# A feed-forward block whose up projection goes by seven products of halves, with the down projection as a stage of its own

## The chip, the cores and the metric

The kernel runs on one core of a Trainium2 chip. The metric is the device time of one execution in microseconds (us). TensorE (PE) multiplies, VectorE (DVE), ScalarE (ACT) and GpSimd (POOL) do the elementwise work, SyncE (SP) issues most DMAs. Each engine runs its own queue in order and waits on semaphores for the others.

## The reference

One layer of a bidirectional RWKV-7 and mLSTM trunk, on 128 context tokens and 1024 latent tokens, which the kernel handles as 1152 columns. The change is in the last part of the layer alone, the gated feed-forward; all before it (modulation, input projection, the two scans, branch and output projections) computes the same as it did.

```
h = rmsnorm(x, norm_g[2]) * (1 + sc2) + sh2                  # (tokens, 1024)
u_act, u_val = split(h @ ffn_up, 2)                          # ffn_up (1024, 2 * 2816)
u_act = dwconv_grid(u_act, ffn_conv) + ffn_conv_b            # 3x3 on a 16x64 grid; width 3 on the context
f = (silu(u_act) * u_val) @ ffn_down                         # ffn_down (2816, 1024)
x = x + g2 * rmsnorm(f, norm_g[3])
```

## The kernel before

The 1152 tokens are 9 blocks of 128, and 3 groups of 384 columns. All large products are made with numbers split in two: `hi` is the value rounded to the matmul's format (an ACT copy), `lo` is what is left (a subtraction on DVE), and a product is hi·hi + hi·lo + lo·hi, three matmuls where one would stand (`mm_split`). `split_w` (L366 to L382) loads a weight tile and makes its two parts.

The output projection (`wo`, L1456 to L1493) takes the blocks one after another: 48 matmuls into two PSUM banks, then a norm, the residual, a second norm, eight transposes, and `modulate` (L1434 to L1454), which writes the hi and lo parts of h, channel-major, into `AS`, where the feed-forward reads them.

The feed-forward has 22 blocks of 128 hidden features. For each block `up_act` (L1510 to L1524) makes 3 x 24 matmuls of 384 columns, two ACT evacuations per group, the convolution on DVE (`conv_taps`, L34 to L50: eight shifted multiply-adds over the grid, "taps", and two small ones over the context), and SiLU on ACT. `up_val` (L1526 to L1536) makes the other 3 x 24 matmuls, multiplies them on DVE straight from PSUM with the activated half, and splits the result into `f2`. The down projection runs in rounds of one to three blocks: 9 token blocks x 2 halves, three matmuls of 512 columns for each block of the round, added to `acc` in SBUF by DVE (L1597). In the last round POOL multiplies `acc` by the gate row (L1599), and norm, residual and output follow. Eight small modulation products (`mod_cols`) stand between the rounds.

A scheduler sets each engine's order from dependencies and program order, except where the code holds an engine to program order (`pe.on`, `v.on`). POOL has nothing to do in the feed-forward until the last round.

## Time and profile before

| | us |
|---|---|
| median of 3 runs (range) | 2232.75 (2231.03 to 2235.47) |
| the profiled execution | 2232.55 |
| its span | 2230.8 |
| last matmul of the output projection starts | 1388.50 |
| last matmuls of the feed-forward start | 2219.47 |

The span runs from the first to the last instruction of the profiled execution; the 1.75 us between it and that execution's time lie outside. The feed-forward is what follows 1388.7 us. In the rows below, busy time of PE and of its weight loads (PEld) overlap, and a matmul's length in a row is longer than its distance from the next, since matmuls are pipelined: rates are read from start to start.

### The profile page before, as it was taken

What the parts mean: (1) busy time and instruction counts of PE and PEld (TensorE: products, weight loads), DVE (VectorE), ACT (ScalarE), POOL (GpSimd) and SP (SyncE); (2) the same over time, 40 slices, a digit from 0 to 9 for tenths busy, and PEclk for the clock granted to TensorE, in tenths of its full rate; (3) what the DMA queues carried; (4) which work ended last, traced back from release to release, by engine and by line L of the source; (5) the groups of instructions that cost most, each with busy time, mean ns of one, the idle gap of its engine ahead of it and who ended that gap; (6) DMA issues with size and microseconds to landing.
All of it is one profiled execution on the core that took longest, in us unless ns stands there. A gap on an engine that the chain in (4) does not pass through costs nothing. (4 is left out here: it accounts for less than half of the span.)

```text
span 2230.8 us, 39173 instructions
## 1 busy us (share of the span) xinstructions
PE 2086.4 (94%) x16051; PEld 1926.7 (86%) x16051; DVE 1372.8 (62%) x2131; ACT 819.8 (37%) x1595; POOL 567.0 (25%) x726
## 2 busy tenths in 40 slices
PE   6999998998988988879879999999999999999998
PEld 4998998988877877869868888999999999999996
DVE  4766678879744656653733465665575556565658
...
GB/s 268 54 87 127 113 128 106 154 120 138 158 133 139 127 133 133 104 212 214 197 242 194 201 188 75 49 57 57 38 48 57 48 48 48 57 39 47 39 57 170
DMA packets 370803, 256.63 MB, mean 115 GB/s; under 512 B 90529, under 2 KB 345669, under 8 KB 370624
## 3 DMA queue, kind: packets, MB, share of 16 engines
...
## 5 line engine op out<-in xcount | busy, mean ns | idle before, releaser
L395 PE MATMUL pg<-act,whi 128*128 128x384 f32 (+1 forms) x3808 | 727.0, 338 | 0.5 <-DVE act L358 0.4
L395 PEld LDWEIGHTS pg<-act,whi 128*128 128x128 f32 (+1 forms) x3808 | 667.6, 188 | 12.9 <-DVE act L358 0.8
L395 PE MATMUL pg<-act,wlo 128*128 128x384 f32 (+1 forms) x1904 | 373.8, 336 | 5.1 <-DVE wlo L382 5.1
L395 PEld LDWEIGHTS pg<-act,wlo 128*128 128x128 f32 (+1 forms) x1904 | 333.4, 187 | 8.6 <-DVE wlo L382 5.4
L382 DVE TENSOR_TENSOR wlo<-wraw,whi 128x1024 fp32r<-128x1024 f32 x130 | 164.2, 1264 | 227.8 <-ACT whi L381 222.1
L47 DVE SCALAR_TENSOR_TENSOR ua<-uraw,par,ua 128x945 f32<-128x945 f32 (+2 forms) x176 | 215.0, 1221 | 39.2 <-ACT ua L1519 36.0
L1599 POOL TENSOR_TENSOR x<-facc,grow 128x512 f32<-128x512 f32 x16 | 23.5, 1488 | 809.1 <-DMA x<-x1d 799.0
L395 PE MATMUL pfd<-whi,f 128*128 128x512 f32 x792 | 226.1, 394 | 0.2 <-ACT f L1533 0.2
L381 ACT ACTIVATE whi<-wraw 128x1024 fp32r<-128x1024 f32 x130 | 136.7, 1053 | 156.4 <-PE pg L395 85.3
L395 PEld LDWEIGHTS pfd<-whi,f 128*128 128x128 f32 x792 | 147.0, 188 | 28.9 <-issue 1.6
L1597 DVE TENSOR_TENSOR facc<-pfd,facc 128x512 f32<-128x512 f32 x162 | 110.8, 690 | 50.5 <-PE pfd L395 50.5
L542 POOL TENSOR_TENSOR Lb<-Lb,tmp 96x31 f32<-96x31 f32 (+15 forms) x155 | 129.4, 835 | 12.2
L540 POOL TENSOR_TENSOR tmp<-La,Lb 96x31 f32<-96x31 f32 (+15 forms) x155 | 121.9, 787 | 28.7 <-DMA La<-Ad 16.9
L395 PE MATMUL pfd<-wlo,f 128*128 128x512 f32 x396 | 122.7, 391 | 0.0
L1523 ACT ACTIVATE ua<-ua 128x1152 f32<-128x1152 f32 x22 | 25.7, 1168 | 221.8 <-DVE ua L47 221.8
L1533 ACT ACTIVATE f<-ua 128x384 fp32r<-128x384 f32 x66 | 32.0, 518 | 192.9 <-DVE ua L1532 192.9
L69 PE MATMUL pg<-act,whi 128*128 128x384 f32 x496 | 99.3, 349 | 0.0
L1467 PE MATMUL pwo<-whi,act 128*128 128x512 f32 x288 | 90.1, 392 | 1.1 <-ACT whi L381 1.1
L874 DVE TENSOR_TENSOR KA<-psc,msk 64x512 f32<-64x512 f32 x72 | 49.3, 684 | 67.2 <-ACT A L873 66.0
L47 DVE SCALAR_TENSOR_TENSOR qacc<-zraw,par,qacc 128x945 f32<-128x945 f32 (+2 forms) x64 | 84.4, 1319 | 9.5 <-ACT qacc L598 9.0
L395 PEld LDWEIGHTS pfd<-wlo,f 128*128 128x128 f32 x396 | 74.3, 188 | 16.5
L69 PEld LDWEIGHTS pg<-act,whi 128*128 128x128 f32 x496 | 87.3, 194 | 1.1
...
## 6 DMA issues: line engine op xcount, KB each, us to landing
...
```

Of the source, the lines that this page charges most:

```text
L47: v.scalar_tensor_tensor(o, img[:, r0 + i:r1 + i, c0 + j:c1 + j], wt, o, op0=ALU.mult, op1=ALU.add)
L69: return (lambda *a, **k: tc.keep_in_program_order(f(*a, **k))) if self.on else f
L381: s.activation(hi, raw, AF.Copy)
L382: v.tensor_tensor(lo, raw, hi.bitcast(F32), op=ALU.subtract)
L395: pe.matmul(out, wt(hw, k), at(ha, k), start=(i == 0), stop=(i == last))
L540: e.tensor_tensor(t3, L[:, j, i].unsqueeze(2).to_broadcast([NI, n, m]), X[:, j:j + 1, c].to_broadcast([NI, n, m]), op=ALU.mult)
L542: e.tensor_tensor(X[:, i, c], X[:, i, c], t3, op=ALU.subtract)
L874: v.tensor_tensor(q.KA[orr, :, h, :], sc_[h][orr], msk[orr, d:d + 1, :].to_broadcast([64, 4, 128]), op=ALU.mult)
L1467: pe.matmul(pts[b][q], AS[g][:, ha, k, 128 * o:128 * o + 128], wo2[k][hw][:, 0, 512 * q:512 * q + 512], start=(k == 0 and i == 0), stop=(k ...
L1523: s.activation(ua, ua, AF.Silu)
L1533: s.activation(f2[:, 0, gs], ua[:, gs], AF.Copy)
L1597: v.tensor_tensor(acc[:, b, qs], pt, acc[:, b, qs], op=ALU.add)
```

## The change

The last step of the output projection no longer writes hi and lo parts but stores h itself in memory (`h2d`). From there the feed-forward loads it in two chunks of 576 tokens. Each chunk is one step of Strassen's recursion in Winograd's form: h is cut into four quarters (two halves of the channels, two of the tokens, 288 columns each), the weights of a feature block into four (two halves of the channels; the activation and the value features), and seven products P1 to P7 of quarters or of their sums and differences stand in place of eight. The operand sums on the token side (T1 to T4) are made once for all blocks; those on the weight side are made on POOL for every block; the output sums are made by DVE and POOL as the products leave PSUM. Every product ("unit") is 12 matmuls of 288 columns.

The convolution runs as before, a step after each unit. The product of the two halves is made on POOL, and stored to memory (`f2d`) from POOL's queue. When all blocks are done, the down projection runs in three sweeps of 384 tokens that keep their sums in PSUM: it loads f back from `f2d` (`f_group`), splits it, and loads `ffn_down` (13 of its 22 row blocks in every sweep, the other 9 once). The eight `mod_cols` move into the output projection, and all eight PSUM banks belong to the units.

```diff
+    h2d = dram("h2d", [2, 128, 4, T])
+    f2d = dram("f2d", [NFB, 128, T])
...
+    def x_load(c, q, t, dst):
+
+        o = 2 * TH * c + TH * t
+        dma(f32(dst), h2d[q][:, :, o:o + TH])
...
+    def x_split(c, nm, raw, hi, lo):
+        s.activation(hi, f32(raw), AF.Copy)
+        v.tensor_tensor(lo, f32(raw), f32(hi), op=ALU.subtract)
+        X[nm, c] = (hi, lo)
...
+    def x_sub(e, out, a, b):
+        e.tensor_tensor(out, f32(a), f32(b), op=ALU.subtract)
+        return out
...
-            hi = AS[g][:, 0, 4 * q:4 * q + 4, 128 * o:128 * o + 128]
-            lo = AS[g][:, 1, 4 * q:4 * q + 4, 128 * o:128 * o + 128]
-            s.activation(hi, hf, AF.Copy)
-            (v if b == NB - 1 else gp).tensor_tensor(lo, hf, hi.bitcast(F32), op=ALU.subtract)
-
-    with tc.tile_pool(name="wo", bufs=1) as wop, tc.tile_pool(name="wot", bufs=2) as wt:
+            dma(h2d[q][:, :, 128 * b:128 * b + 128], hf)
...
+                modulate(ob, b)
+                if b > 0:
+
+                    for _ in mod_cols(128 * (39 + b), 128, (8,), aw_, wt, pss):
+                        pass
+            if b == 5:
+
+                x0 = actp.tile([128, 6144], F32R, name="x0", tag="act0")
+                x1 = actp.tile([128, 6144], F32R, name="x1", tag="act1")
+                r11, r12, r21, r22, x22l = (quarter(x0, i) for i in range(5))
+                x11h, x11l, x21h, x21l, x22h = (quarter(x1, i) for i in range(5))
+                for q, t, r in ((0, 0, r11), (1, 0, r21), (0, 1, r12), (1, 1, r22)):
+                    x_load(0, q, t, r)
+                x_split(0, "X11", r11, x11h, x11l)
+                x_split(0, "X21", r21, x21h, x21l)
+                x_split(0, "X22", r22, x22h, x22l)
+                ta = x_sub(gp, x_tmp(), r12, r11)
+                tb = x_sub(gp, x_tmp(), r22, ta)
...
+    banks(pg=8)
...
+    def x_rest(c, ta, tb, raw, his):
+
+        r11, r12, r21, r22 = raw
+        x_split(c, "T1", ta, his[0], r11)
+        tc_ = x_sub(v, x_tmp(), r22, r12)
+        x_split(c, "T2", tb, his[1], r22)
+        td = x_sub(v, tb, tb, r21)
+        x_split(c, "T3", tc_, his[2], r12)
+        x_split(c, "T4", td, his[3], r21)
+
+    x_rest(0, ta, tb, (r11, r12, r21, r22), [quarter(x2, i) for i in range(4)])
+    q11, q12, q21, q22 = xb[4:8]
+    x_load(1, 0, 0, q11)
+    x_load(1, 1, 0, q21)
+    x_split(1, "X11", q11, xb[1], xb[2])
+    x_split(1, "X21", q21, xb[3], xb[8])
+    x_load(1, 0, 1, q12)
+    x_load(1, 1, 1, q22)
+
+    def x_late():
+        x_split(1, "X22", q22, xb[9], xb[10])
+        ta = x_sub(v, x_tmp(), q12, q11)
+        tb = x_sub(v, x_tmp(), q22, ta)
+        x_rest(1, ta, tb, (q11, q12, q21, q22), [xb[0]] + xb[11:14])
...
+    PROD = ("P1", "P2", "P6", "P7", "P4", "P5", "P3")
+    XOP = dict(P1="X11", P2="X21", P6="T2", P7="T3", P4="T4", P5="T1", P3="X22")
+
+    units = [(0, "P1", 0), (0, "P2", 0), (0, "P1", 1), (0, "P2", 1), (0, "P6", 0), (0, "P7", 0),
+             (1, "P1", 0), (1, "P2", 0), (1, "P1", 1), (1, "P2", 1), (0, "P4", 0), (0, "P5", 0),
+             (0, "P6", 1), (0, "P7", 1), (0, "P4", 1), (0, "P5", 1), (0, "P3", 0), (0, "P3", 1)]
+    units += [(1, m, c) for m in PROD[2:] for c in range(2)]
+    units += [(i, m, c) for i in range(2, NFB) for m in PROD for c in range(2)]
...
+    def w_split(i, m):
+
+        a11, a12, a21, a22 = raws[i]
+        if m == "P1":
+            s1s[i] = wt.tile([128, 4, 128], F32, name="s1", tag="hf", bufs=1)
+        s1 = s1s[i]
+        src = dict(P1=a11, P2=a12, P6=a11, P7=a21, P4=a22, P5=s1, P3=a12)[m]
+        w = hl()
+        s.activation(w[:, 0], src, AF.Copy)
+        (gp if m in ("P5", "P3") else v).tensor_tensor(w[:, 1], src, f32(w[:, 0]), op=ALU.subtract)
+        HLs[i, m] = w
+        if m == "P1":
+            gp.tensor_tensor(s1, a21, a22, op=ALU.add)
+            gp.tensor_tensor(a21, a11, a21, op=ALU.subtract)
+            gp.tensor_tensor(a11, s1, a11, op=ALU.subtract)
+        if m == "P2":
+            gp.tensor_tensor(a12, a12, a11, op=ALU.subtract)
+
...
+        def unit(i, m, c):
+
+            w, x = HLs[i, m], X[XOP[m], c]
+            t1 = slice(2 * TH * c, 2 * TH * c + TH)
+            t2 = slice(2 * TH * c + TH, 2 * TH * c + 2 * TH)
+            pt = psg([128, TH], "pu")
+            n = 0
+            for hw, hx in PARTS:
+                for k in range(4):
+                    pe.matmul(pt, w[:, hw, k], x[hx][:, k], start=(n == 0), stop=(n == 11))
+                    n += 1
+            if m == "P1" and c == 0:
+                acts[i] = cvt("uraw")
+            if m == "P7" and c == 0:
+                vals[i] = cvt("uval")
+            act, val = acts[i], vals.get(i)
+            if m == "P1":
+                s.activation(act[:, t2], pt, AF.Copy)
+            elif m == "P2":
+                s.activation(act[:, t1], pt, AF.Copy)
+                gp.tensor_tensor(act[:, t1], act[:, t1], act[:, t2], op=ALU.add)
+            elif m == "P6":
+                v.tensor_tensor(act[:, t2], pt, act[:, t2], op=ALU.add)
+            elif m == "P7":
+                v.tensor_tensor(val[:, t2], pt, act[:, t2], op=ALU.add)
+            elif m == "P4":
+                v.tensor_tensor(val[:, t1], val[:, t2], pt, op=ALU.subtract)
+            elif m == "P5":
+                v.tensor_tensor(val[:, t2], pt, val[:, t2], op=ALU.add)
+                v.tensor_tensor(act[:, t2], pt, act[:, t2], op=ALU.add)
+            else:
+                v.tensor_tensor(act[:, t2], pt, act[:, t2], op=ALU.add)
...
+        def conv(i):
+
+            raw, val = acts.pop(i), vals.pop(i)
+            ua = cvt("ua")
+            s.activation(ua, raw, AF.Identity, scale=P("ffn_conv", 22 * 4 + i), bias=P("ffn_conv_b", i))
+            yield
+            for _ in conv_taps(v, raw, ua, lambda t: P("ffn_conv", 22 * t + i)):
+                yield
+            s.activation(ua, ua, AF.Silu)
+            gp.tensor_tensor(val, val, ua, op=ALU.mult)
+            pdma(f2d[i], val)
+            yield
...
+        def f_group(sw, j):
+
+            n = min(8, NFB - 8 * j)
+            t_ = actp.tile([128, 2, 8, G3], F32R, name="fg", tag=f"act{(1, 0, 2)[j]}")
+            ts = slice(G3 * sw, G3 * sw + G3)
+            for o in range(0, n, 2):
+                dma(f32(t_[:, 1, o:o + 2]), f2d[8 * j + o:8 * j + o + 2, :, ts].rearrange("k p t -> p k t"))
+                s.activation(t_[:, 0, o:o + 2], f32(t_[:, 1, o:o + 2]), AF.Copy)
+                v.tensor_tensor(t_[:, 1, o:o + 2], f32(t_[:, 1, o:o + 2]), f32(t_[:, 0, o:o + 2]), op=ALU.subtract)
+                yield
...
+        for u, (i, m, c) in enumerate(units):
+            while ns < len(order) and first_of[order[ns]] <= u + 9 and (ns < 6 or last_of[order[ns - 6]] < u):
+                w_split(*order[ns])
+                ns += 1
+                j = nloaded[0]
+                if j < NFB and all((j - 2, p_) in HLs for p_ in PROD):
+                    w_load()
+            if u == 6:
+                x_late()
+            unit(i, m, c)
+            if conving:
+                next(conving, None)
+            if (m, c) == ("P3", 1):
+                if conving:
+                    for _ in conving:
+                        pass
+                conving = conv(i)
+            if (i, m, c) == (NFB - 1, "P7", 1):
+                g0 = f_group(0, 0)
...
+        for sw in range(3):
+            pd = [[psg([128, 512], "pfd") for q in range(2)] for o in range(3)]
...
+            no = NFB - 3 if sw == 0 else NS
+            for k in range(no):
...
+                w = wds.pop(k) if k < NS else res[k]
+                for o in range(3):
                     for q in range(2):
+                        down_mm(pd[o][q], sw, k, o, q, w, k == 0, False)
...
+                    for k in range(no, NFB):
+                        down_mm(pd[o][q], sw, k, o, q, res[k], False, k + 1 == NFB)
+                    out_half(b, q, pd[o][q], ob, ss)
...
+                out_norm(b, x, ob, ss)
```

POOL, first before, then now. Before, its last rows are the gate products of the branch merge (L1415), the lo parts of h in the output projection (L1454) and the gate products of the last round (L1599):

```order
L1415 TENSOR_TENSOR sg_13402<-sg_13402,sg_13404 128x384 x3
L1454 TENSOR_TENSOR act_160<-hf,act_160 128x4x128 x6
L1454 TENSOR_TENSOR act_161<-hf,act_161 128x4x128 x6
L1454 TENSOR_TENSOR act_162<-hf,act_162 128x4x128 x4
L1599 TENSOR_TENSOR x_20292<-facc,grow 128x512 x6
L1599 TENSOR_TENSOR x_20293<-facc,grow 128x512 x6
L1599 TENSOR_TENSOR x_20294<-facc,grow 128x512 x4
```

Now one block's period in the middle of the feed-forward reads so (`hl` are the hi and lo parts of a weight quarter, `s` and `wraw` the weight quarters and their sums, `uraw` and `uval` the two halves of the block's outputs):

```order
L1623 TENSOR_TENSOR hl<-s_15709,hl 128x512
L1626 TENSOR_TENSOR s_15956<-wraw 128x512
L1627 TENSOR_TENSOR wraw<-wraw 128x512
L1623 TENSOR_TENSOR hl<-wraw,hl 128x512
L1658 TENSOR_TENSOR uraw<-uraw 128x288 x2
L1628 TENSOR_TENSOR wraw<-s_15956,wraw 128x512
L1630 TENSOR_TENSOR wraw<-wraw 128x512
L1680 TENSOR_TENSOR uval<-uval,ua 128x1152
L1681 DMA f2d<-uval 128x1152
```

POOL has ten instructions in every block of the feed-forward, where it had none.

DVE, first before, a stretch between two rounds (`facc` is the down projection's sum):

```order
L47 SCALAR_TENSOR_TENSOR ua<-uraw,par,ua 128x15x63
L47 SCALAR_TENSOR_TENSOR ua<-uraw,par,ua 128x16x63 x2
L47 SCALAR_TENSOR_TENSOR ua<-uraw,par,ua 128x15x63
L47 SCALAR_TENSOR_TENSOR ua<-uraw,par,ua 128x960
L47 SCALAR_TENSOR_TENSOR ua<-uraw,par,ua 128x15x63
L1532 TENSOR_TENSOR ua<-pg,ua 128x384 x3
L1534 TENSOR_TENSOR f_16144<-ua,f_16144 128x384 x3
L382 TENSOR_TENSOR wlo<-wraw,whi 128x1024
L50 SCALAR_TENSOR_TENSOR ua<-uraw,par,ua 128x127 x2
L382 TENSOR_TENSOR wlo<-wraw,whi 128x1024
L47 SCALAR_TENSOR_TENSOR ua<-uraw,par,ua 128x15x63
L266 TENSOR_TENSOR modT<-pmt,par 128x2
```

and now, from the last of a block's output sums on (`pu` is PSUM):

```order
L1669 TENSOR_TENSOR uraw<-pu,uraw 128x288 x2
L47 SCALAR_TENSOR_TENSOR ua<-uraw,par,ua 128x15x63
L50 SCALAR_TENSOR_TENSOR ua<-uraw,par,ua 128x127
L47 SCALAR_TENSOR_TENSOR ua<-uraw,par,ua 128x960
L50 SCALAR_TENSOR_TENSOR ua<-uraw,par,ua 128x127
L47 SCALAR_TENSOR_TENSOR ua<-uraw,par,ua 128x15x63
L47 SCALAR_TENSOR_TENSOR ua<-uraw,par,ua 128x16x63 x2
L1660 TENSOR_TENSOR uraw<-pu,uraw 128x288
L1623 TENSOR_TENSOR hl<-wraw,hl 128x512
L47 SCALAR_TENSOR_TENSOR ua<-uraw,par,ua 128x15x63
L1660 TENSOR_TENSOR uraw<-pu,uraw 128x288
L1623 TENSOR_TENSOR hl<-wraw,hl 128x512
```

The sums of the down projection have gone from between the taps; output sums of 288 columns from PSUM and lo parts of weight quarters have come. The first tap of a block stands right behind the last output sum of that block.

PE at the end of the output projection, before:

```order
L1467 MATMUL pwo<-whi,act_162 128x512 x2
L1467 MATMUL pwo<-wlo,act_162 128x512
L1467 MATMUL pwo<-whi,act_162 128x512
L395 MATMUL pg<-act_160,whi 128x384 x16
L395 MATMUL pg<-act_160,wlo 128x384 x8
L395 MATMUL pg<-act_161,whi 128x384 x10
L1441 MATMUL ptx<-ident,ob 128x128 x8
L395 MATMUL pg<-act_161,whi 128x384 x6
L395 MATMUL pg<-act_161,wlo 128x384 x8
```

and now:

```order
L1499 MATMUL pwo<-whi,act_164 128x512 x2
L1499 MATMUL pwo<-wlo,act_164 128x512
L1499 MATMUL pwo<-whi,act_164 128x512
L1473 MATMUL ptx<-ident,ob 128x128 x8
L258 MATMUL pmod<-aw,sc 32x128 x8
L267 MATMUL pmt<-sel,mrow 128x2
L70 MATMUL pu<-x_14216,hl 128x288 x24
L70 MATMUL pu<-xb_14566,hl 128x288 x4
L70 MATMUL pu<-xb_14567,hl 128x288 x4
```

Matmuls of the up projection stood between the last matmul of the output projection and the last block's transposes (`ptx`); now transposes, `pmod` and `pmt` come first.

DVE in the same place, before, from the last block's evacuation on:

```order
L1483 TENSOR_TENSOR ob<-pwo,grow_13533 128x512 x2
L1485 TENSOR_TENSOR rso<-sso 128x1
L319 RECIPROCAL rso<-rso 128x1
L1487 SCALAR_TENSOR_TENSOR xt_14379<-ob,rso,xt_14379 128x1024
L319 RECIPROCAL s2o<-s2o 128x1
L1492 TENSOR_SCALAR ob<-xt_14379,s2o 128x1024
L1449 TENSOR_SCALAR hf<-ptx,sc_13524,modT 128x128 x4
L1454 TENSOR_TENSOR act_162<-hf,act_162 128x4x128 x2
```

and now:

```order
L1516 TENSOR_TENSOR ob<-pwo,grow_13538 128x512
L1518 TENSOR_TENSOR rso<-sso 128x1
L1455 TENSOR_TENSOR x_14215<-xs,x_14565 128x1152
L322 RECIPROCAL rso<-rso 128x1
L1463 TENSOR_TENSOR xs<-x_14215 128x1152
L1520 SCALAR_TENSOR_TENSOR xt_14496<-ob,rso,xt_14496 128x1024
L1455 TENSOR_TENSOR x_14215<-xs,x_14565 128x1152 x2
L1463 TENSOR_TENSOR xs<-xs,x_14215 128x1152
L322 RECIPROCAL s2o<-s2o 128x1
L1455 TENSOR_TENSOR xb_14567<-xb_14569,xb_14566 128x1152
L1525 TENSOR_SCALAR ob<-xt_14496,s2o 128x1024
L1455 TENSOR_TENSOR x_14215<-xs,x_14565 128x1152
```

Operations of 1152 columns on the token operands (`x`, `xs`, `xb`) stand within the chain that ends in the last block's normalised rows (`ob`, L1525 now).

## Rows read from the trace of the kernel before

**Rows 1.** Windows: stretch, its length, busy time (instructions) of each engine, granted clock, DMA.

```profile
core 0: us, PE busy (x) PEld busy (x) DVE busy (x) ACT busy (x) POOL busy (x), PEclk, DMA share, GB/s
1100.00:1150.00 50.00, 39.51 (x240) 37.25 (x238) 29.78 (x75) 19.98 (x47) 7.10 (x9) 1.00 0.72 245
...
1388.70:2220.30 831.60, 831.37 (x4509) 777.16 (x4507) 510.73 (x637) 221.67 (x350) 22.94 (x16) 1.00 0.18 56
```

**Rows 2.** Timeline of PE: start, length, engine, line, operation, out<-in, count.

```profile
1439.71 0.62 PE L395 MATMUL pfd<-whi,f 128*128 128x512 f32 x2
...
1440.39 0.62 PE L395 MATMUL pfd<-whi,f 128*128 128x512 f32 x2
...
1445.42 2.93 PE L395 MATMUL pg<-act,whi 128*128 128x384 f32 x16
...
1449.58 2.93 PE L395 MATMUL pg<-act,whi 128*128 128x384 f32 x16
```

**Rows 3.** Timeline of DVE in the feed-forward stage, with the idle time before a row.

```profile
1402.83 2.36 DVE L382 TENSOR_TENSOR wlo<-wraw,whi 128x1024 fp32r<-128x1024 f32 x2 [1.15 <-ACT whi L381]
...
1467.51 10.03 DVE L47 SCALAR_TENSOR_TENSOR ua<-uraw,par,ua 128x945 f32<-128x945 f32 x8 [0.16 <-ACT ua L1519]
1478.84 1.49 DVE L1532 TENSOR_TENSOR ua<-pg,ua 128x384 f32<-128x384 f32 x3 [1.30 <-ACT ua L1523]
...
1484.44 0.74 DVE L50 SCALAR_TENSOR_TENSOR ua<-uraw,par,ua 128x127 f32<-128x127 f32 x2 [1.57 <-ACT ua L1519]
...
1496.56 0.69 DVE L1597 TENSOR_TENSOR facc<-pfd,facc 128x512 f32<-128x512 f32 x1
1497.16 1.26 DVE L47 SCALAR_TENSOR_TENSOR ua<-uraw,par,ua 128x1008 f32<-128x1008 f32 x1
```

**Rows 4.** Two POOL lines: engine, operation, count, shortest/median/longest ns, first and last start.

```profile
L1599 POOL TENSOR_TENSOR x<-facc,grow x16: 1289/1301/1748, 2186.9 to 2219.2; 128x512 f32<-128x512 f32 x16
...
L1415 POOL TENSOR_TENSOR sg<-sg,sg x24: 997/1015/1928, 1166.1 to 1279.9; 128x384 f32<-128x384 f32 x24
```

**Rows 5.** Timeline of DVE and POOL in the last 35 us.

```profile
2196.34 3.00 POOL L1599 TENSOR_TENSOR x<-facc,grow 128x512 f32<-128x512 f32 x2 [1.29 <-DVE facc L69]
...
2196.78 3.11 DVE L69 SCALAR_TENSOR_TENSOR x<-x,ss 128x512 f32<-128x512 f32 x2
...
2223.87 1.41 DVE L69 SCALAR_TENSOR_TENSOR x<-x,ss 128x512 f32<-128x512 f32 x2
```

**Rows 6.** Timelines of DVE and of POOL in the output projection.

```profile
1327.91 1.39 DVE L1483 TENSOR_TENSOR ob<-pwo,grow 128x512 f32<-128x512 f32 x2
1329.21 1.27 DVE L1485 TENSOR_TENSOR rso<-sso 128x1 f32<-128x1 f32 x1
...
1327.32 1.29 POOL L1454 TENSOR_TENSOR act<-hf,act 128x512 fp32r<-128x512 f32 x1 [4.27 <-ACT act L1453]
1329.17 1.30 POOL L1454 TENSOR_TENSOR act<-hf,act 128x512 fp32r<-128x512 f32 x1 [0.56 <-ACT act L1453]
```

**Rows 7.** Timeline where the output projection ends and the feed-forward begins.

```profile
1388.50 0.39 PE L1467 MATMUL pwo<-whi,act 128*128 128x512 f32 x1
...
1388.72 2.96 PE L395 MATMUL pg<-act,whi 128*128 128x384 f32 x16
...
1394.81 1.09 PE L1441 MATMUL ptx<-ident,ob 128*128 128x128 f32 x8
```

**Rows 8.** One line of DVE: 1152 columns, shortest/median/longest ns.

```profile
L1390 DVE TENSOR_TENSOR y2r<-y2r x4: 1358/1359/1360, 1128.6 to 1134.3; 128x1152 fp32r<-128x1152 f32 x4
```

**Rows 9.** Timeline of PE: one modulation block of the eight in the feed-forward.

```profile
1491.28 0.65 PE L255 MATMUL pmod<-aw,sc 128*32 128x128 f32 x16
...
1492.90 0.28 PE L264 MATMUL pmt<-sel,mrow 128*128 128x2 f32 x2
```

**Rows 10.** Timeline, the end: PE's last matmuls, the last output write.

```profile
2219.47 0.84 PE L395 MATMUL pfd<-whi,f 128*128 128x512 f32 x3
...
2227.41 0.36 ACTq L1562 DMA_DIRECT2D y_sample<-x  x1
```

More of the change, by code (lines that the diff above doesn't have):

```diff
@@ L1492, in _body @@
                 v.tensor_scalar(ob, xt, s2, None, op0=ALU.mult)
-                modulate(wt, ob, b, sc2, sh2, AS)
-    if "h2T" in dbg:
-        for g in range(3):
-            for q in range(2):
-                dma(dbg["h2T"][q, :, :, G3 * g:G3 * g + G3], AS[g][:, q].bitcast(F32))
+                modulate(ob, b)
[14 more added lines that the diff above has]
+                tb = x_sub(gp, x_tmp(), r22, ta)
+        rows_out(1, make_scale("g2", 40, 3, 0.0))
     if stop == "h2":
@@ new lines, in _body @@
+    banks(pg=8)
+    fx = pool("fx", 1, fst)
+    x2 = actp.tile([128, 6144], F32R, name="x2", tag="act2")
+    xb = [quarter(x2, 4)] + [quarter(fx.tile([128, 4 * TH], F32R, name=f"xb{i}"), 0) for i in range(13)]
+    def x_rest(c, ta, tb, raw, his):
[6 more added lines that the diff above has]
+        x_split(c, "T4", td, his[3], r21)
@@ new lines, in _body, with w_load @@
+    order, last_of, first_of = [], {}, {}
+    for n, (i, m, c) in enumerate(units):
+        if (i, m) not in first_of:
+            first_of[i, m] = n
+            order.append((i, m))
+        last_of[i, m] = n
+    raws, HLs, s1s, nloaded, nhl = {}, {}, {}, [0], [0]
+    def w_load():
+        i = nloaded[0]
+        nloaded[0] += 1
+        ra, rv = (wp.tile([128, 8, 128], F32, name="wraw", tag="wlo", bufs=4) for _ in range(2))
+        dma(ra, kp(up[:, 128 * i:128 * i + 128]))
+        dma(rv, kp(up[:, DFF + 128 * i:DFF + 128 * i + 128]))
+        raws[i] = (ra[:, 0:4], ra[:, 4:8], rv[:, 0:4], rv[:, 4:8])
```

213 lines of the change are left out of this document (111 added, 102 removed).

## The prediction

> **What bounds the kernel now.** I read the windows of the stages first. From 1388.7 to 2220.3 us PE is busy 831.37 of 831.60 us at a granted clock of 1.00, while DVE is busy 510.73 and POOL 22.94 [rows 1]: the feed-forward costs what its matmuls cost. The timeline of PE gives their rates from start to start. The 24 matmuls of 384 columns that begin at 1445.42 end where the next 24 begin, 4.16 us later, so 173.3 ns each; two with hi weights and one with lo, of 512 columns, take 0.68 us, so 226.7 ns [rows 2]. A straight line through both is 13.3 ns + 0.4167 ns a column. Up is 22 x 6 x 24 = 3168 x 173.3 = 549.1 us, down 22 x 18 x 3 = 1188 x 226.7 = 269.3 us; the eight modulation products are 0.65 + 0.28 each [rows 9], 7.4 us; with the last block's transposes, 1.1 [rows 7], that is 826.9, and 4.7 of waits are left. The tail from 2220.3 to the span's end at 2230.8 is 10.5 us [rows 10]. After 1388.7 the kernel spends 842.1 us.
>
> **PE's work in the change.** 22 blocks x 14 units x 12 = 3696 matmuls of 288 columns. On the line they are 133.3 ns, 492.8 us in all, 56 us less: a unit is 1.60 us, a block 22.4. The line is an estimate below 384 columns. From above, the weight load could hold it: eight transposes of 128 columns, each with its load, took 1.09 us with their latency [rows 7], 136 ns each at most, so a block is at most 22.9. From below, 0.75 x 173.3 = 130 ns gives 21.8. I take 22.4. The down products are the same, 269.3.
>
> **DVE's work per block.** The taps are 10.03 + 0.74 = 10.8 us [rows 3]. Five lo parts of 512 columns: two of 1024 took 2.36, so about 0.60 each, 3.0. Twelve output sums of 288 columns from PSUM: three of 384 took 1.49, with a last latency in it, and one of 512 is followed after 0.60 [rows 3], so 0.37 each, 4.4. The first tap stands right behind the last output sum of the same block and needs ACT's pass over 1152 columns; the same kind of wait is 1.30 today [rows 3]. Together 19.5 us, under 22.4. Alone, DVE would be hidden under PE.
>
> **POOL's work per block, and what it costs DVE.** An operation of 512 columns is 1.29 us, one of 384 is 1.00 [rows 4]; on that line 288 columns are 0.78 and 1152 are 2.74. Six, two and one make 12.0 us. POOL itself has the time. But its operands and the taps' are all in SBUF. Where this happened before, two DVE operations with two SBUF inputs took 3.11 us beside two POOL operations that took 3.00; the same two alone took 1.41 [rows 5], and the POOL pair alone is 2.58. From 2196.34 to 2199.89 all four took 3.55, only 0.44 less than one after another. So a POOL operation of 512 columns takes 1.29 - 0.22 = 1.07 us from DVE, one of 288 takes 0.56, one of 1152 takes 2.5: 10.0 us per block. A DVE operation that reads PSUM is free of it: two of 512 columns took 1.39 while POOL worked from 1327.32 to 1328.61 [rows 6].
>
> Bounds for the block: all hidden, 22.4 (PE). POOL's 10.0 and DVE's 10.8 + 3.0 never at once, the rest covered: 23.8. Nothing covered: 19.5 + 10.0 = 29.5. I walk through one block in the printed order to choose. Where POOL runs under output sums or the 1.3 us wait, it is free. The lo part of P5 falls under four P5 sums: 0. `s1`, right behind it: 1.1. `a21`, partly under the P3 sums: 0.4. The lo part of P3 starts under the wait, and with the two adds costs 0.8 in the taps. `a11` and `a12` meet taps and lo parts: 1.5. The product of 1152 columns has one output sum beside it: 2.5 - 0.4 = 2.2. Sum 6.0, so 25.5 us, 3.1 over PE. PE then waits for the hi and lo parts and for banks; a clock of 1.00 held in a stretch with PE 79% busy (39.51 of 50) [rows 1], so I take no loss there.
>
> The rule of the Trainium skill that bears on this ("SBUF — State Buffer", section "Who interferes with whom") says that a DVE instruction with two SBUF inputs and a GpSimd instruction that reads SBUF contend, and that the shared ports go to one for the whole instruction while the other blocks. The 128x1 operation that took 1.27 us and ended with POOL's [rows 6] agrees with it; the 0.44 us of overlap [rows 5] does not quite. By the rule the nine POOL operations hold 12.0 us, not 10.0, and the time would be near 2289 instead of 2259.
>
> **Start of the up stage.** PE used to have up matmuls beside the last block's norm: transposes began 6.3 us after the last output matmul started, at 1394.81 [rows 7]. Now transposes, `pmod` and `pmt` stand ahead of the first unit, so this wait shows. And DVE's order puts six subtractions of 1152 columns into the chain that ends in `ob`. One takes 1.36 us [rows 8], about 1.27 from start to start: 7.6. So 6.3 + 7.6 + 1.1 = 15.0 us of idle PE. Below: if DVE does the six while it would wait for ACT or the load, 7; above, with POOL's token sums beside them, 20. The moved modulation products add their 7.4 to the output projection, whose PE is the limit there, and three lo parts of 1152 columns at block 5 some 3. In blocks 0 and 1 there are no taps yet for most of the time, but DVE makes the token operands; 28 units x 1.6 + 3 = 48.
>
> **Between up and down, and after.** The first f loads are queued on SP behind a weight load that waits for a late product, and the last block's f must go out and come back: 5 us with PE idle (0 to 15). A sweep of 90 us loads about 11 MB, 125 GB/s, where 245 GB/s has been moved [rows 1]; I add 4 us in the first sweep for the last store, 273.3 in all (269 to 300). The tail loses the separate sum and gate product, about 4 of 10.5: 6.6.
>
> **Sum** after 1388.7: 7.4 + 3 + 15 + 48 + 20 x 25.5 + 5 + 273.3 + 6.6 = 868.3, against 842.1. Span 2257.0; with the 1.75 us outside it 2258.8. The profiled execution, 2232.55, is 0.2 below the median, 2232.75, so no correction: 2259 us, 1.2% slower. PE saves 56; the block's overrun gives back 62 (20 x 3.1), the start and the seams the rest.
>
> **Rivals.**
> *Other side, faster: POOL is covered.* Every term but the block's stays; a block below 25.5 - 26.2 / 20 = 24.2 us turns the sign. At 23.8 the time is 2225, at PE's 22.4 it is 2197. For it: POOL has 22.4 us for 12.0, each engine slides to where the other is free, and up to eight banks let PE run on while DVE is late. Against it: 23.8 needs every output sum and the whole wait to lie over POOL's work, while DVE waits for PE in some of them, and the two queues are fixed in order; the product of 1152 columns waits for DVE's last tap. 0.27.
>
> *The whole-instruction hold.* Each POOL operation costs its full length; the uncovered part grows by 1.5 to 27.0 a block: 2289. For it the 1.27 us operation [rows 6], against it the four operations in 3.55 [rows 5]. 0.14. The rule named above is this case.
>
> *Next to nothing is covered:* 28.0 to 29.5 a block, 2309 to 2339. It needs ACT, too, to come late with hi parts, so that the five lo parts stand in DVE's way; ACT is busy 221.67 of 831.60 [rows 1], which speaks against it. 0.08.
>
> *The seams cost it:* blocks near 24 but the down sweeps wait for f and weights on SP's queue, 20 to 30 us more than I gave: 2250 to 2260 by another way. 0.05, without effect on the bounds.
>
> **Chances.** Forecast 0.46, its own range 2235 to 2285 (block 24.3 to 26.8). The range 2195 to 2310 takes in PE's floor, the port floor and the full hold; what is left out is most of the fourth case and a little below 2195. About 0.2% (4.5 us) is what a measurement of this kernel tells from no change. Faster, below 2228: the covered case but for 0.03 of it, 0.24. Within, 2228 to 2237: that 0.03 and 0.05 from the forecast's lower end, 0.08. Slower: the rest of the forecast, 0.41, and the three other cases, 0.27, so 0.68.
>
> **What would show it.** Right: in the middle of up, PE busy about 88%, a block's period near 25.5, DVE busy nearly throughout; taps (L47) beside POOL at 2 us and more, 1.25 without; output sums (L1660 to L1669) at their 0.4 to 0.5 whatever POOL does; PE idle some 15 us before the first unit; down with PE near full. Wrong: PE busy above 97% in up (POOL is covered), or matmuls of 288 columns not 133 ns apart, or a clock under 1.00 there, or a down stage far over 273 us.

## The result and the profile after

The changed kernel takes 2304.11 us (median of 4 runs, 2297.62 to 2305.92), the kernel before 2234.1 (4 runs): a ratio of 1.031, 95% interval 1.0286 to 1.0334. It is slower by 70 us, where 26 were forecast. The direction, and the block's period to the tenth, were right; the stages around the blocks were not.

The profiled execution of the changed kernel took 2297.62 us, the fastest of the four, with a span of 2295.9. Its windows answer to [rows 1]: the output projection, the wait for the first unit, blocks 0 and 1, the other 20 blocks, the seam, the down sweeps, the tail.

```profile
core 0: us, PE busy (x) PEld busy (x) DVE busy (x) ACT busy (x) POOL busy (x), PEclk, DMA share, GB/s
1278.50:1401.60 123.10, 118.94 (x621) 92.85 (x622) 59.74 (x107) 51.61 (x116) 5.89 (x2) 0.97 0.61 195
1401.60:1419.00 17.40, 3.94 (x28) 2.67 (x26) 16.41 (x23) 12.00 (x21) 0.00 (x0) 0.59 0.32 104
1419.00:1475.50 56.50, 50.46 (x336) 49.52 (x337) 41.50 (x48) 19.03 (x30) 27.96 (x20) 0.89 0.37 76
1475.50:1982.30 506.80, 463.59 (x3362) 445.99 (x3360) 467.82 (x534) 148.87 (x257) 291.93 (x196) 1.00 0.20 64
1982.30:1991.10 8.80, 0.22 (x2) 0.00 (x0) 8.19 (x14) 4.94 (x6) 3.23 (x2) 0.65 0.61 185
1991.10:2289.50 298.40, 280.34 (x1188) 226.49 (x1188) 117.76 (x138) 89.56 (x121) 5.51 (x2) 0.96 0.46 156
2289.50:2295.90 6.40, 0.34 (x2) 0.00 (x0) 2.17 (x4) 0.98 (x3) 0.00 (x0) 0.70 0.22 82
```

Their lengths beside the terms of the prediction:

| | forecast us | measured us |
|---|---|---|
| start of the output projection | 1280.4 (as before) | 1278.5 |
| output projection | 118.5 (108.1 + 7.4 + 3) | 123.1 |
| last output matmul to first unit | 15 | 17.4 |
| blocks 0 and 1 | 48 | 56.5 |
| 20 blocks | 510 | 506.8 |
| seam | 5 | 8.8 |
| down | 273.3 | 298.4 |
| tail | 6.6 | 6.4 |

The 20 blocks took 506.8 us and not 20 x 25.55, because the first of them still ran at 22.17 and the last took 24.8. In the 20 blocks PE is busy 91% and DVE 92%, and what PE waits for is DVE's output sums:

```profile
PE pu L70 <- DVE uraw L1667: 28.2, 19, 1.5
PE pu L70 <- DVE uval L1662: 9.1, 17, 0.6
PE pu L70 <- DVE uraw L1660: 5.4, 19, 0.9
```

(what waits, for what: us in all, times, the longest). The timeline of DVE in one block, and POOL's under it, show the price that [rows 5] foretold (`a12` is POOL's row of L1630, `a11` that of L1628, the product that of L1680; the two rows of L1658 are the adds):

```profile
1701.87 2.16 DVE L47 SCALAR_TENSOR_TENSOR ua<-uraw,par,ua 128x960 f32<-128x960 f32 x1
...
1704.32 1.19 DVE L47 SCALAR_TENSOR_TENSOR ua<-uraw,par,ua 128x945 f32<-128x945 f32 x1
...
1705.80 0.68 DVE L1623 TENSOR_TENSOR hl<-wraw,hl 128x512 fp32r<-128x512 f32 x1
...
1707.32 2.77 DVE L1623 TENSOR_TENSOR hl<-wraw,hl 128x512 fp32r<-128x512 f32 x1 [0.48 <-ACT hl L1622]
1710.01 0.44 DVE L1666 TENSOR_TENSOR uval<-pu,uval 128x288 f32<-128x288 f32 x1
...
1714.45 1.38 DVE L47 SCALAR_TENSOR_TENSOR ua<-uraw,par,ua 128x945 f32<-128x945 f32 x1 [1.42 <-ACT ua L1675]
1715.76 1.38 DVE L50 SCALAR_TENSOR_TENSOR ua<-uraw,par,ua 128x127 f32<-128x127 f32 x1
1717.06 1.76 DVE L47 SCALAR_TENSOR_TENSOR ua<-uraw,par,ua 128x960 f32<-128x960 f32 x1
```

```profile
1698.92 2.11 POOL L1628 TENSOR_TENSOR wraw<-s,wraw 128x512 f32<-128x512 f32 x1 [4.98 <-DVE hl L1623]
1701.72 1.29 POOL L1630 TENSOR_TENSOR wraw<-wraw 128x512 f32<-128x512 f32 x1 [0.69 <-DVE hl L1623]
1706.85 2.69 POOL L1680 TENSOR_TENSOR uval<-uval,ua 128x1152 f32<-128x1152 f32 x1 [3.83 <-ACT ua L1679]
...
1715.61 1.38 POOL L1623 TENSOR_TENSOR hl<-wraw,hl 128x512 fp32r<-128x512 f32 x1 [0.77 <-ACT hl L1622]
1716.95 2.54 POOL L1658 TENSOR_TENSOR uraw<-uraw 128x288 f32<-128x288 f32 x2
```

A tap is 1.19 us alone (945 columns) and 2.16 beside `a12` (960 columns); a lo part is 0.68 alone and 2.77, so 2.1 more, beside the product. It ends 0.55 us after the product does: it hardly moved while POOL worked. A context tap (L50), 0.37 each in [rows 3], takes 1.38 beside P3's lo part. Output sums from PSUM stay at 0.44. PE's unit period is 22.17/14 = 1.58 us (see e1), and a block takes 25.55.

In the down stage PE stops several times. The longest stop, from PE's timeline; then the queue of SP and what it waited for longest but for PE (us in all, times, the longest); then POOL:

```profile
2026.57 1.22 PE L70 MATMUL pfd<-whi,fg 128*128 128x512 f32 x2 [9.04 <-ACT whi L1706]
```

```profile
2000.29 4.43 SPq L76 DMA_DIRECT2D wraw<-in_ffn_down  x2
2016.10 0.80 SPq L76 DMA_DIRECT2D grow<-grd  x2
2017.00 0.38 SPq L76 DMA_DIRECT2D wraw<-in_ffn_down  x1
2025.16 0.37 SPq L76 DMA_DIRECT2D fg<-f2d  x1
```

```profile
SPq L76 <- POOL uval L1680: 11.3, 1, 11.3
SPq L76 <- DMA f2d<-uval: 7.7, 1, 7.7
```

```profile
2011.16 4.92 POOL L1680 TENSOR_TENSOR uval<-uval,ua 128x1152 f32<-128x1152 f32 x1 [23.19 <-ACT ua L1679]
```

SP's queue ends its weight loads at 2004.7 and does nothing until 2016.1, when POOL's last product ends (2011.16 + 4.92 = 2016.08): the gate rows `grow` wait for that product (in the code their pool opens when that of the product's tiles closes) and stand ahead of the next weight load. Then the last pair of `fg` waits for the last block's store until 2025.16, again ahead of weight loads. After such stops PE runs at half clock for a while: windows behind the first stop and around the long one. The last three rows are the three sweeps, whose matmuls alone are 89.8 us each.

```profile
1994.00:1998.40 4.40, 4.40 (x11) 3.43 (x12) 4.40 (x6) 2.53 (x4) 0.00 (x0) 0.50 1.05 393
1998.40:2016.90 18.50, 18.04 (x78) 14.34 (x77) 12.98 (x13) 6.51 (x8) 5.45 (x2) 1.00 0.21 72
2016.90:2026.50 9.60, 0.64 (x3) 0.19 (x1) 0.00 (x0) 1.03 (x1) 0.06 (x1) 0.79 0.79 228
2026.50:2032.70 6.20, 6.08 (x14) 4.35 (x15) 2.18 (x2) 0.87 (x2) 0.00 (x0) 0.50 0.97 375
...
1991.10:2102.60 111.50, 97.64 (x396) 77.39 (x397) 58.42 (x64) 43.35 (x53) 5.51 (x2) 0.92 0.57 193
2102.60:2198.80 96.20, 92.47 (x397) 75.13 (x396) 31.19 (x39) 24.74 (x36) 0.00 (x0) 0.98 0.46 157
2198.80:2289.50 90.70, 90.23 (x397) 73.97 (x396) 28.15 (x36) 21.47 (x33) 0.00 (x0) 1.00 0.32 108
```

### The profile page after: what moved, and what is told of

Its sections match the earlier page's. It is cut to its first block, busy times and chain, and to the rows that moved or that the text cites. A ratio compares the mean times of both kernels' runs of the same rounds, so it can differ in the third digit from the quotient of the medians.

```text
span 2295.9 us, 41348 instructions
## 1 busy us (share of the span) xinstructions
PE 2062.2 (90%) x16579; PEld 1876.9 (82%) x16579; DVE 1498.9 (65%) x2219; ACT 878.6 (38%) x1702; POOL 856.5 (37%) x916
## 4 chain that ended last, share of the span: by engine, by line
PE 43%; DVE 27%; DMA 12%; issue 9%; ACT 6%; POOL 1%; SPq 1%; DVEq 0%; ACTq 0%; POOLq 0%
PE pg L398 10%; PE pfd L70 10%; DVE ua L47 8%; PE pwo L1499 4%; PE pbr L70 4%; PE pg L70 4%; PE pu L70 2%; DVE ua L50 2%; PE pY L70 1%; ACT ua L1675 1%; DMA aw<-in_ada_w 1%; SPq L76 1%; DMA wraw<-in_ffn_down 1%; PE pmN L70 1%; DMA bon<-bond 1%
## 5 line engine op out<-in xcount | busy, mean ns | idle before, releaser
L398 PE MATMUL pg<-act,whi 128*128 128x384 f32 (+1 forms) x1696 | 329.6, 342 | 0.9 <-DVE act L361 0.4
L70 PE MATMUL pu<-x,hl 128*128 128x288 f32 x2024 | 299.9, 298 | 30.0 <-DVE uraw L1667 27.3
L70 PEld LDWEIGHTS pu<-x,hl 128*128 128x128 f32 x2024 | 277.1, 189 | 39.1 <-issue 31.6
L398 PEld LDWEIGHTS pg<-act,whi 128*128 128x128 f32 (+1 forms) x1696 | 297.5, 189 | 7.8 <-DVE act L361 0.8
L70 PE MATMUL pu<-xb,hl 128*128 128x288 f32 x1672 | 252.1, 298 | 20.1 <-DVE uval L1662 9.1
L70 PEld LDWEIGHTS pu<-xb,hl 128*128 128x128 f32 x1672 | 231.0, 190 | 29.6 <-DVE uval L1662 13.5
L398 PE MATMUL pg<-act,wlo 128*128 128x384 f32 (+1 forms) x848 | 168.7, 338 | 8.4 <-DVE wlo L385 8.4
L70 PE MATMUL pfd<-whi,fg 128*128 128x512 f32 x468 | 150.2, 403 | 23.6 <-ACT whi L1706 13.0
L398 PEld LDWEIGHTS pg<-act,wlo 128*128 128x128 f32 (+1 forms) x848 | 147.9, 186 | 12.1 <-DVE wlo L385 8.7
L1623 DVE TENSOR_TENSOR hl<-wraw,hl 128x512 fp32r<-128x512 f32 x110 | 135.6, 1233 | 16.6 <-ACT hl L1622 16.4
L543 POOL TENSOR_TENSOR tmp<-La,Lb 96x31 f32<-96x31 f32 (+15 forms) x155 | 124.8, 805 | 28.9 <-DMA La<-Ad 17.1
L545 POOL TENSOR_TENSOR Lb<-Lb,tmp 96x31 f32<-96x31 f32 (+15 forms) x155 | 126.8, 818 | 12.2
L1680 POOL TENSOR_TENSOR uval<-uval,ua 128x1152 f32<-128x1152 f32 x22 | 61.5, 2795 | 103.9 <-ACT ua L1679 103.9
```

The lines of the kernel that those rows point to most:

```text
L70: return (lambda *a, **k: tc.keep_in_program_order(f(*a, **k))) if self.on else f
L398: pe.matmul(out, wt(hw, k), at(ha, k), start=(i == 0), stop=(i == last))
L543: e.tensor_tensor(t3, L[:, j, i].unsqueeze(2).to_broadcast([NI, n, m]), X[:, j:j + 1, c].to_broadcast([NI, n, m]), op=ALU.mult)
L545: e.tensor_tensor(X[:, i, c], X[:, i, c], t3, op=ALU.subtract)
L1623: (gp if m in ("P5", "P3") else v).tensor_tensor(w[:, 1], src, f32(w[:, 0]), op=ALU.subtract)
L1680: gp.tensor_tensor(val, val, ua, op=ALU.mult)
```

## The experiments

Theory: in the blocks, POOL's operations hold up DVE's two-operand work, and the rest of the loss is waits in queue order at the seams. Rivals: DVE is full by itself or waits in its own chain; the down loads are limited by DMA throughput. The stages of all runs, read from the starts of the first and last matmuls of a kind (the period is the mean from the start of block 5 to that of block 20):

| run | output projection | last output matmul to block 2 | period | last up to last down matmul | median us |
|---|---|---|---|---|---|
| changed kernel | 123.1 | 73.9 | 25.55 | 307.2 | 2304.11 |
| e1_pool_fill | 125.8 | 70.8 | 22.17 | 293.7 | 2227.18 |
| e2_mult_dve | 123.6 | 74.7 | 25.31 | 301.0 | 2293.09 |
| e3_down_queue | 125.5 | 75.0 | 25.55 | 298.8 | 2301.27 |
| e4_start_order | 123.0 | 74.2 | 25.54 | 306.1 | 2308.07 |
| e5_rebalance | 126.2 | 72.9 | 22.23 | 296.3 | 2230.21 |
| e6_seams | 125.7 | 74.0 | 25.55 | 293.6 | 2294.65 |
| e7_both | 124.8 | 72.8 | 22.58 | 294.8 | 2234.12 |
| e8_rebalance_seams | 123.0 | 72.8 | 22.25 | 289.6 | 2231.66 |
| e9_rebalance_start | 125.8 | 77.2 | 22.20 | 298.9 | 2237.22 |
| e10_all_three | 125.3 | 77.0 | 22.20 | 295.3 | 2230.26 |

The kernel before had medians of 2234.3 to 2234.6 beside them. The last output matmul starts anywhere from 1401.6 (the changed kernel's profile, the earliest) to 1419.5 us (e8's); part of that lies in stages that no edit here touches. So edits worth a few us are judged by stages, not by the median.

**e1_pool_fill**

```diff
+    def fill(t_):
+        for _ in range(2):
+            gp.memset(t_, 0.0)
...
-            gp.tensor_tensor(a21, a11, a21, op=ALU.subtract)
+            fill(a21)
```

The same is done for all nine operations.

> POOL's nine operations per block are replaced by two fills each of the same destination: POOL stays busy and in its place, but reads nothing from SBUF. The weight sums, two adds, two lo parts and the product are left out of the computation. Theory (POOL's reads keep DVE's second SBUF operand out, 6 us a block): a block's period falls from 25.54 to PE's 22.4, give or take 0.4, taps are 1.25 us throughout, and the time falls by 20 x 3.1 = 62 to about 2240. Rival 1 (DVE's own work and the waits between PE, ACT and DVE set the period, POOL is a bystander): the period stays within 0.5 of 25.5 and the time near 2300. Rival 2 (POOL itself is late with the weight sums): the same as rival 1 as long as POOL's fills take about as long as its operations did.

The period is 22.17, so PE's 12 matmuls of a unit take 1.58 us, 132 ns each (133.3 forecast). Windows of 200 us, and the taps in them (shortest/median/longest):

```profile
1600.00:1800.00 200.00, 200.00 (x1517) 200.00 (x1516) 160.53 (x245) 73.52 (x118) 91.69 (x173) 1.00 0.23 75
```

```profile
L47 DVE SCALAR_TENSOR_TENSOR ua<-uraw,par,ua x74: 1187/1205/1270, 1599.0 to 1799.9; 128x945 f32<-128x945 f32 x36, 128x1008 f32<-128x1008 f32 x20, 128x960 f32<-128x960 f32 x18
```

POOL is still busy 46% (58% in the 20 blocks above; a fill of 512 columns takes 0.53 us, two stand for 1.29), but no tap exceeds 1.27 us, PE never waits, and 3.4 us a block are gone. That is the theory; both rivals said 25.5. The fills also wait for no operands, so this run alone would leave open whether DVE had waited for late results of POOL; the changed kernel's trace answers that, where DVE's only listed waits in a block are 1.4 and 0.5 us, both for ACT, so at most the 0.5 could go back to POOL. The run also gives DVE's own work: 160.5 us in 200, so 17.8 a block, and 1.5 of the wait for ACT, 19.3 where 19.5 was forecast. The Trainium skill, "SBUF — State Buffer", section "Who interferes with whom", says that two-input DVE work contends with a GpSimd instruction that reads SBUF and not with one that only writes it: the run agrees.

**e2_mult_dve**

```diff
-            gp.tensor_tensor(val, val, ua, op=ALU.mult)
+            v.tensor_tensor(val, val, ua, op=ALU.mult)
```

> The product of 1152 columns goes from POOL to DVE. DVE is the engine that sets the period, and gets 1.3 us more work per block. Theory: on POOL the product costs DVE 2.2 us that nothing covers, on DVE 1.3, so the period falls by 0.9 to 24.6 and the time by 18 to about 2285. Rival (DVE is simply full, POOL's work costs it nothing): the period rises by 1.3 to 26.8, the time by 26 to about 2330.

A ratio of 1.0264 (1.0239 to 1.0289) and a period of 25.31: 0.24 less instead of 0.9 less or 1.3 more. The rival falls, since DVE got 1.36 us more work and the block still became shorter. The gain is smaller than forecast, but not because the product had cost DVE less: the lo part beside it was 2.1 us longer (see above), near the 2.2 of the forecast. POOL's other operations moved in time and now meet more of DVE's work. An estimate over twelve blocks of each trace, DVE's lengths less the median lengths of the same forms in e1 (0.68 for a lo part, 1.20 to 1.27 for a tap, 0.34 for a context tap): DVE's operations were longer by 6.2 us a block in the changed kernel, 4.1 of them beside POOL's other operations, and are longer by 4.9 here, all beside the others.

The last block's product is early, too, and with SP's queue in its old order the 9 us stop is gone: the longest stop at a weight load is 1.6 us, and the down stretch is 6 us shorter. That speaks for the wait on SP independently of e3.

**e3_down_queue**

```diff
-            dma(t_, grd[i, c:c + 1, :].to_broadcast([128, D]))
+            (dma, pdma)[i](t_, grd[i, c:c + 1, :].to_broadcast([128, D]))
...
-                dma(f32(t_[:, 1, o:o + 2]), f2d[8 * j + o:8 * j + o + 2, :, ts].rearrange("k p t -> p k t"))
+                (pdma if (sw, j, o) == (0, 2, 4) else dma)(f32(t_[:, 1, o:o + 2]), f2d[8 * j + o:8 * j + o + 2, :, ts].rearrange("k p t -> p k t"))
...
-                dma(x, x1d[b])
+                (dma if sw else pdma)(x, x1d[b])
```

> The gate rows, the last pair of f in the first sweep and the residual rows of the first sweep are issued from POOL's queue instead of SP's, where they stood ahead of weight loads and waited for the last block's product and its store. Theory (head-of-line waits on SP starve the down stage): the stop of 9.6 us at 2016.9, the 2.0 us at half clock after it and half of the stops up to 2055 go, 12 to 18 us, and the time falls to about 2288. Rival (the loads are limited by DMA throughput, which is at 350 to 390 GB/s around the stops): the stops only move, and the time changes by less than 4 us.

The stretch falls by 8.4 us, between the theory's 12 to 18 and the rival's under 4. The median falls by 2.8 us only, and not to the 2288 expected, but within a few us it does not judge (above). The three transfers were moved together, so the run does not tell them apart. What is left of the long stop has moved to another engine's queue. ACT and PE in its timeline:

```profile
2037.36 0.84 ACT L1695 ACTIVATE fg<-fg 128x768 fp32r<-128x768 f32 x1 [9.99 <-DMA fg<-f2d]
2038.11 1.99 ACT L1706 ACTIVATE whi<-wraw 128x1024 fp32r<-128x1024 f32 x2
...
2039.20 1.22 PE L70 MATMUL pfd<-whi,fg 128*128 128x512 f32 x2 [4.54 <-ACT whi L1706]
```

The copy of the last f pair, which PE needs only for blocks 20 and 21, stands on ACT ahead of the weight copies that PE needs now.

**e4_start_order**

```diff
+            v.on = blocks[0] == NB - 1
             pts = {b: [psg([128, 512], "pwo") for q in range(2)] for b in blocks}
...
     x_load(1, 1, 1, q22)
+    v.on = False
```

> DVE is held to program order for the last block of the output projection and the token operands of the first chunk, so the six operations of 1152 columns come behind the chain that ends in ob. Theory: the time between the last output matmul and the first unit falls from 17.4 us by 6 x 1.3 = 7.8 to about 9.6, and since the second chunk's load hangs on the same chain, most of it stays: the time falls by 5 to 8 us. Rival (the operands are needed as early as before, so the wait moves behind the fourth unit): the first unit starts 8 us earlier, but the second block of the up stage ends at the same time, and the whole time changes by less than 3 us.

The first unit comes 3.6 us earlier (13.8 after the last output matmul), not 7.8: in this trace ACT's passes over the token operands (2.21 and 1.16 us, L1454) stand in the same chain, ahead of the two small operations that the norms wait for. And block 2 starts no earlier. PE's timeline:

```profile
1422.53 4.78 PE L70 MATMUL pu<-x,hl 128*128 128x288 f32 x24 [0.34 <-DVE modT L70]
1438.07 2.29 PE L70 MATMUL pu<-xb,hl 128*128 128x288 f32 x8 [10.24 <-DVE xb L70]
```

The wait moved behind the first units: the rival holds.

**e5_rebalance**

```diff
-        (gp if m in ("P5", "P3") else v).tensor_tensor(w[:, 1], src, f32(w[:, 0]), op=ALU.subtract)
+        (gp if m == "P5" else v).tensor_tensor(w[:, 1], src, f32(w[:, 0]), op=ALU.subtract)
...
-            gp.tensor_tensor(a11, s1, a11, op=ALU.subtract)
+            v.tensor_tensor(a11, s1, a11, op=ALU.subtract)
...
-            gp.tensor_tensor(a12, a12, a11, op=ALU.subtract)
+            v.tensor_tensor(a12, a12, a11, op=ALU.subtract)
...
-                s.activation(act[:, t1], pt, AF.Copy)
-                gp.tensor_tensor(act[:, t1], act[:, t1], act[:, t2], op=ALU.add)
+                v.tensor_tensor(act[:, t1], pt, act[:, t2], op=ALU.add)
...
-            gp.tensor_tensor(val, val, ua, op=ALU.mult)
+            v.tensor_tensor(val, val, ua, op=ALU.mult)
```

> Of POOL's nine operations per block three stay (lo of P5, s1, a21, which stand beside output sums and the wait before the first tap); the lo part of P3, a11, a12 and the product go to DVE, and the two adds with them, as sums straight from PSUM (ACT's copy of P2 goes). Theory (what POOL does beside two-operand DVE work costs DVE more than the same work on DVE): from 25.31 with the product moved, the stretched taps and lo parts give back 3.8 us and the moved work adds 3 x 0.6 + 2 x 0.37 = 2.5, so the period is 24.0, the time about 2265. Rival (DVE's own work sets the period): it rises by 2.5 from 25.3 to 27.8 and the time goes to about 2340.

Further than the theory: a mean of 22.23, and a ratio of 0.9988 (0.9972 to 1.0004), no different from the kernel before. 400 us of its windows, and DVE's timeline where the wait before the first tap stood, with the same last output sum (L1668 at 1710.77) two and three blocks on:

```profile
1500.00:1900.00 400.00, 399.99 (x3025) 398.93 (x3024) 400.00 (x592) 124.95 (x197) 93.89 (x72) 1.00 0.23 74
```

```profile
1710.77 0.44 DVE L1668 TENSOR_TENSOR uraw<-pu,uraw 128x288 f32<-128x288 f32 x1
1711.13 1.43 DVE L1623 TENSOR_TENSOR hl<-wraw,hl 128x512 fp32r<-128x512 f32 x1
1712.48 0.44 DVE L1657 TENSOR_TENSOR uraw<-pu,uraw 128x288 f32<-128x288 f32 x1
1712.85 1.86 DVE L47 SCALAR_TENSOR_TENSOR ua<-uraw,par,ua 128x945 f32<-128x945 f32 x1
...
1755.45 0.45 DVE L1668 TENSOR_TENSOR uraw<-pu,uraw 128x288 f32<-128x288 f32 x1
...
1777.81 0.45 DVE L1668 TENSOR_TENSOR uraw<-pu,uraw 128x288 f32<-128x288 f32 x1
```

A lo part and the new sum of P2 now stand behind the last output sum, so the 1.42 us wait of the changed kernel is filled. The 24.0 had kept it; 24.0 - 1.4 = 22.6. DVE got more operations and has no idle time in these 400 us; that it comes out so short is because what it does now runs mostly unstretched (1.4 us a block longer by the estimate of e2, for 4.9 there). But DVE is still the limit: its own period is 22.35 (from 1710.77 to 1755.45 and to 1777.81, two and three blocks). PE runs 13 blocks at its own 22.17 on the lead that it has over DVE, and the last seven at 22.3 to 22.4.

**e6_seams** (with the edits of e3)

```diff
-            t_ = actp.tile([128, 2, 8, G3], F32R, name="fg", tag=f"act{(1, 0, 2)[j]}")
+            t_ = actp.tile([128, 2, 8, G3], F32R, name="fg", tag=f"act{(2, 0, 1)[j]}")
...
+                s.on = sw == 0 and k >= 6
                 if k in (2, 6):
-                    for _ in f_group(sw, 1 + k // 6):
-                        pass
+                    fgen = f_group(sw, 1 + k // 6)
+                    for n_, _ in enumerate(fgen):
+                        if (sw, k, n_) == (0, 6, 1):
+                            break
+                if (sw, k) == (0, 14):
+                    for _ in fgen:
+                        pass
```

(Of ACT and DVE, which the text below names, only ACT was held to an order.)

> As e3, and two more edits in the down stage: the first f group goes to the tile that the up stage frees two units earlier, and ACT and DVE are held to an order in which the last f pair of the first sweep is split just before it is used. Theory (the stops are head-of-line waits, in e3 the last f pair's copy stood on ACT ahead of weight copies): the 5.1 us stop of e3 goes, the wait before the first down matmul falls from 8.9 to about 5, and from the last up matmul to the last down matmul it takes about 288 us (307 in the changed kernel, 299 in e3); the time is about 2286. Rival (DMA throughput): the stops move again and the same stretch stays within 3 us of e3's 299.

293.6, halfway between 299 and 288: e3's 5 us stop is gone and the seam is 6.8 us. What remains over the 269.3 us of the matmuls is 24.3: the seam, some 11 us in stops of 0.6 to 2.2 us at weight loads, nearly all in the first two sweeps, and matmuls at a lower clock in the first (0.95). The order of transfers and copies, with the earlier tile, accounts for 13.6 of the 307.2. What holds up the remaining loads is not shown. The three sweeps move 208, 159 and 108 GB/s here, well under the 375 to 393 of the short windows above, which speaks against throughput as the limit of a whole sweep, but no run tried it.

**e7_both** (the edits of e5 and e6, and:)

```diff
-            s.activation(ua, raw, AF.Identity, scale=P("ffn_conv", 22 * 4 + i), bias=P("ffn_conv_b", i))
+            for h_ in (slice(0, 2 * TH), slice(2 * TH, 4 * TH)):
+                s.activation(ua[:, h_], raw[:, h_], AF.Identity, scale=P("ffn_conv", 22 * 4 + i), bias=P("ffn_conv_b", i))
```

> e5 and e6 together, and ACT's pass before the first tap in two halves of 576 columns, so that the first tap waits for half of it. Theory: the period is 23.4 (24.0 less half of the 1.3 us wait), still over PE's 22.2, so DVE still sets it; the time is 2304 less 21 x 2.1 for the period and less 19 for the seams, about 2241, still no faster than the kernel before by more than the noise. Rival (the contention was all that kept PE waiting): the period is PE's 22.2 and the time about 2215.

The period is 22.58, 0.35 more than in e5: the halves changed the order that the scheduler gave DVE, and there was no wait left to shorten. Behind the last output sum there now stand the two context taps, which take 2.41 us beside POOL's work (0.34 each in e5). Ratio 0.9989 (0.9971 to 1.0008). Its expectation was written before e5 was known; neither number of it was met.

**e8_rebalance_seams** (the edits of e5 and e6)

> e5 with the down-stage edits of e6, without the halved pass of e7. Theory (in e7 the two halves changed DVE's order and cost 0.35 a block; the pass needs no halves, since in e5 other DVE work stands in front of the first tap): the period is 22.2 as in e5, the stretch from the last up matmul to the last down matmul 293 as in e6 (296 in e5), the time about 2227. Rival (the shorter up stage leaves the down stage's first loads less time): the period is 22.2, the stretch stays at 296 or more, and the time at 2230 or above.

Period 22.25 and a stretch of 289.6, 6.7 less than e5's. Ratio 0.9976 (0.9959 to 0.9994): faster than the kernel before by 0.24%, barely more than can be told, and than the changed one by far. The median of 2231.66 misses the 2227. Of the kernels that compute the whole layer it is the fastest by its ratio.

**e9_rebalance_start** (the edits of e5 and e4, and:)

```diff
-    x_rest(0, ta, tb, (r11, r12, r21, r22), [quarter(x2, i) for i in range(4)])
...
     x_load(1, 1, 1, q22)
+    x_rest(0, ta, tb, (r11, r12, r21, r22), [quarter(x2, i) for i in range(4)])
```

> e5 with DVE held to program order around the start of the up stage as in e4, but the operands of the second chunk that the third unit needs are split ahead of the first chunk's sums. Theory (in e4 the ten-microsecond wait behind the first units was DVE's order, not the work): the first unit starts 3.6 us earlier than in e5 and no wait of over 3 us follows, so that from the last output matmul to block 2 it takes about 68 instead of 72.9 us. Rival (DVE and ACT have that much work there in any order): this stretch stays at 72 to 74.

77.2 us, worse than either theory: the first unit comes 3.7 us earlier and seven waits follow up to block 2, the longest 5.6. This program order is a worse one than the scheduler's. Ratio 1.0005 (0.9986 to 1.0024).

**e10_all_three**

> e8 and e9 together. Theory: 2230 less 3 for the down stage and less 5 for the start, 2222, 0.5% under the kernel before. Rival: no change from e5 beyond the noise of a few microseconds, 2227 to 2233.

It loses at the start (77.0) and has a longer down stretch than e8 (295.3). Ratio 0.9982 (0.9965 to 0.9999), the second best; 2230.26 lies in the rival's 2227 to 2233, not at the theory's 2222.

## Why the prediction was right and wrong

*PE's work:* right. 22.17 us a block where PE is never kept waiting (e1), 22.4 forecast.

*The blocks:* right. 25.55 for 25.5, with DVE as the limit and the stretch beside POOL as its reason, which e1 took away. The sum of what POOL costs is right, 6.2 for 6.0 by the estimate of e2, but in part by luck. The product cost 2.1 (2.2 forecast), `a11` and `a12` 1.7 (1.5). P3's lo part with the two adds cost 2.2 where 0.8 was given, and `s1`, `a21` and P5's lo part 0.3 where 1.5 was given: two errors that cancel. The alternation of work that would hide POOL did not come; the whole-instruction hold at 27.0 did not either. For a single pair the hold is nearly whole (of its 0.68 us the lo part got through 0.1 in the 2.2 us that it ran beside the product), but in other pairs it was POOL that lost the time, as `a11` with 2.11 us for 1.29, and POOL has time to spare.

*The output projection:* 15.0 more than before instead of 10.4. Its waits are 4.1 us on the transposes of a block and 4.0 on the first weights, against 0.9 and 1.1 before, and its granted clock is 0.97. What brought them was not tried.

*Start and blocks 0 and 1:* 73.9 instead of 63. The first unit came 17.4 us after the last output matmul, for 15. The wait up to the transposes was 12.6 of them, for 13.9; the transposes, `pmod` and `pmt` took 4.9, at a granted clock of 0.50, where 1.1 was counted. The first units run at half clock, too (24 matmuls in 5.9 us), and PE then waits 5.3 us for the second chunk's operands, 4.6 of them at once, and runs another 24 matmuls in 5.8 us. Of the 48 us, 3 stood for all of this behind the first unit's start. e4 and e9 moved this wait and did not remove it; whether another order would is not shown.

*"Between up and down, and after":* this is the step that failed. It gave 5 us to the seam and 4 us to the first sweep. The seam took 8.8; the sweeps took 29 over the 269.3 of matmuls, 21.7 of them in the first and 6.4 in the second. So 28.9 of the 45 us between forecast and median are here. The rival "the seams cost it" had 20 to 30 us for it, but only as a case in place of the slow blocks, at 0.05; both happened at once. The step named one wait (the f loads behind a weight load) and 125 GB/s against 245 as a reason that the rest is hidden. It did not walk SP's order on: the gate rows and the last f pair stand there ahead of weight loads and wait for a product on POOL and for its store. e3 took 8.4 us of it back by queue order alone, e6 13.6 with ACT's order and the tile of the first f group. Nor did the step count the half clock behind each stop. What makes up the other 15 us of the 28.9 is stops at weight loads and clock, as far as the trace of e6 shows; why those loads are late stays open.

So of the 38.9 us between the forecast span of 2257.0 and the measured 2295.9, 25.1 are in the down stage, 3.8 in the seam, 10.9 from the first wait to block 2 and 4.6 in the output projection, less 1.9 at the start of the output projection, 3.2 in the 20 blocks and 0.2 in the tail (the sum is 0.2 off by rounding). The other 6.5 us to the median lie between this profiled execution and the others of the same kernel.

Slower in the end, though PE saves 56 us: the blocks give back 506.8 - 20 x 22.2 = 63 of them, down and seam 38, the start and the output projection the rest. In e8 the first of these is nearly gone, and the kernel is at the time of the one before.
